# Batched matmul: x loaded one batch per transfer in place of two, and other pieces for the first x's last row tile

## The chip, the cores and the metric

The kernel runs on one core of a Trainium2 chip. The core has a matrix engine (TensorE, PE in the profile; its weight loads are PEld), VectorE (DVE), ScalarE (ACT), GpSimd (POOL) and SyncE (SP), an on-chip memory of 128 partitions (SBUF), an accumulator memory (PSUM), and DMA engines that move data between SBUF and the chip's main memory (HBM). The metric is the time of one execution on the device, in microseconds (us); of several runs the median is given.

## The reference

For each of 32 batches a matrix x[b] of 512 x 1024 is multiplied with a matrix weight[b] of 1024 x 768. Inputs and output are float32 in HBM.

```python
def setup_inputs():
    batch, m, k, n = 32, 512, 1024, 768
    return {
        "x": np.random.randn(batch, m, k).astype(np.float32),
        "weight": np.random.randn(batch, k, n).astype(np.float32),
    }

def reference(x, weight):
    return np.matmul(x, weight).astype(np.float32)
```

A batch reads 2 MiB of x and 3 MiB of weight and writes 1.5 MiB of output. Nothing is shared between batches.

## The kernel before

**Tiling.** P is 128. The 512 rows of a batch are dealt to partitions so that partition p holds rows 4p to 4p+3; each of the four row tiles (MT = 4, index mt) takes one of these rows from every partition. The contraction of 1024 is cut into eight parts of 128 (KT = 8, index ko) in the same interleaved way, so a partition's share of x or of weight is one contiguous run in HBM. Products are computed in bfloat16 and accumulated in float32 PSUM. A row tile has 768 output columns; two row tiles (a pair) fill three PSUM banks of 512 columns, and SPLITS says which piece of which tile goes to which bank.

**Loads.** All loads of weights, and of x from batch 1 on, are issued by GpSimd and turn float32 into bfloat16 on the way. `load_w` (line 65) brings one batch's weights in one transfer, in two or three for the last four batches (CHUNKED). `load_pair` (56) brings x of two batches at once: 64 partitions for each, eight rows to a partition; `load_last` (61) brings the odd last batch alone. x of batch 0 comes as float32 from SP's queue (lines 139 to 144): one transfer for row tiles 0 to 2 over all 128 partitions; for row tile 3, sixteen transfers of six partitions each, four partitions apart, and one of 32 partitions.

**Transposes.** PE needs x with the contraction on the partitions. `words` (73) reads pairs of bfloat16 as one float32 word and transposes them on PE, four 128 x 128 transposes into a PSUM tile pt (two buffers); VectorE copies pt to an xT tile in SBUF. In `transpose_pair` (80) one transposed tile holds rows of both batches of a pair, and the copy sorts them apart; both batches' transposes, eight PSUM tiles, are done ahead of the first batch's matmuls, and the results of the second batch are kept in `ready`. `transpose_first` (97) does batch 0 in float32, eight transposes and two copies for each row tile, all four row tiles ahead of its matmuls. `transpose_last` (90) does batch 31.

**Matmuls and stores.** `matmuls` (117) runs two matmuls for each ko and row tile, 64 a batch. `evacuate` (130) copies the three banks of a pair to the output tile: ScalarE, VectorE, ScalarE. Stores of output are issued by GpSimd one batch behind (line 163), those of batches 25 to 27 together at batch 28; the last four batches' stores are issued by SP (167 to 170 and 203).

**Order.** The whole order is written out by hand. Each engine and each queue takes its instructions in the order of the program: for GpSimd the start is w0, x1 with x2, w1, w2, x3 with x4; then in batch b comes w(b+3) (AHEAD = 3), then the store of b-1, and in odd batches, after the transposes, the pair that begins with x(b+4). A load waits until the buffer that it writes is free: w has four buffers, x two (each of a pair), xT six (each of a pair), output seven. The framework puts in the waits, and gives each queue's DMAs eight semaphores in turn.

Of the kernel before, what the change touches and what calls it, by code (L numbers as in the profile page):

```python
# [9 lines left out]
BF16 = mybir.dt.bfloat16  # L10
# [3 lines left out]
def kernel(  # L14
# [6 lines left out]
    nc = tc.nc  # L21
    B, M, K = x.shape
    _, _, N = weight.shape
    P = 128
    MT = M // P
    KT = K // P
    JT = KT // 2
    N2 = 2 * N
    CHUNKED = {B - 4: (4, 4), B - 3: (4, 4), B - 2: (4, 4), B - 1: (4, 2, 2)}
    AHEAD = 3  # L30
# [3 lines left out]
    const = ctx.enter_context(tc.tile_pool(name="const", bufs=1))  # L34
    first_pool = ctx.enter_context(tc.tile_pool(name="first", bufs=1))
    w_pool = ctx.enter_context(tc.tile_pool(name="w", bufs=4))
    x_pool = ctx.enter_context(tc.tile_pool(name="x", bufs=2))
    xT_pool = ctx.enter_context(tc.tile_pool(name="xT", bufs=6))
    out_pool = ctx.enter_context(tc.tile_pool(name="out", bufs=7))
    tpsum = ctx.enter_context(tc.tile_pool(name="tpsum", bufs=2, space=bass.MemoryType.PSUM))  # L40
    mpsum = ctx.enter_context(tc.tile_pool(name="mpsum", bufs=2, space=bass.MemoryType.PSUM))

    w_view = weight.rearrange("b (ki ko) n -> b ki ko n", ki=P)
    x_view = x.rearrange("b (mi mo) k -> b mi mo k", mi=P)
    pair_view = x[1:B - 1].rearrange("(p r) (mi mo) k -> p (r mi) mo k", r=2, mo=2 * MT)
    out_view = out.rearrange("b (mi mo) n -> b mi (mo n)", mi=P)

    xs, ws, outs = {}, {}, {}

    def banks():
        return [mpsum.tile([P, 512], F32, name=f"pm{i}") for i in range(3)]

    def load_pair(b):

        xs[b] = x_pool.tile([P, 2 * MT, K], BF16, name="x_sb")
        nc.gpsimd.dma_start(out=xs[b], in_=pair_view[b // 2])  # L59

    def load_last():
        xs[B - 1] = x_pool.tile([P, MT, K], BF16, name="x_sb")
        nc.gpsimd.dma_start(out=xs[B - 1], in_=x_view[B - 1])  # L63

    def load_w(b):
        ws[b] = w_pool.tile([P, KT, N], BF16, name="w_sb")
        at = 0
        for n in CHUNKED.get(b, (KT,)):
            nc.gpsimd.dma_start(out=ws[b][:, at:at + n, :], in_=w_view[b, :, at:at + n, :])  # L69
            at += n  # L70


    def words(b, mo):
        pt = tpsum.tile([P, JT, P], F32, name="pt")
        pairs = xs[b].bitcast(F32)
        for j in range(JT):
            nc.tensor.transpose(pt[:, j, :], pairs[:, mo, j::JT], ident)  # L77
        return pt.bitcast(BF16)

    def transpose_pair(b, mt):  # L80

        both = xT_pool.tile([P, 2, JT, P // 2, 2, 2], BF16, name="xT")
        for half in range(2):
            nc.vector.tensor_copy(  # L84
                both[:, :, :, :, half, :].rearrange("p b j i r -> p j b i r"),
                words(b, mt + MT * half).rearrange("p j (b i r) -> p j b i r", b=2, r=2),
            )
        return [both[:, r].rearrange("p j i h r -> p j (i h) r") for r in range(2)]

    def transpose_last(mt):  # L90
        xT = xT_pool.tile([P, JT, P, 2], BF16, name="xT")
        nc.vector.tensor_copy(  # L92
            xT.rearrange("p j m r -> p (j m r)"), words(B - 1, mt).rearrange("p j m -> p (j m)")
        )
        return xT

    def transpose_first(mt):

        xT = xT_pool.tile([P, JT, P, 2], BF16, name="xT")
        for h in range(2):  # L100
            pt = tpsum.tile([P, JT, P], F32, name="pt")
            for i in range(JT):
                nc.tensor.transpose(pt[:, i, :], x_first[:, mt, JT * h + i::KT], ident)  # L103
            nc.vector.tensor_copy(  # L104
                xT[:, 2 * h:2 * h + 2].rearrange("p j m r -> p j r m"),
                pt.rearrange("p (j r) m -> p j r m", r=2),
            )
        return xT
# [8 lines left out]
    def matmuls(pm, half, xT, b, kos, together):  # L117
        for ko in kos:
            for i, (bank, at, off, size) in enumerate(SPLITS[half]):
                shares = half == 1 and i == 0  # L120
                nc.tensor.matmul(  # L121
                    pm[bank][:, at:at + size],
                    xT[:, ko // 2, :, ko % 2],
                    ws[b][:, ko, off:off + size],
                    start=(ko == 0 and not (together and shares)),
                    stop=(ko == KT - 1),
                    skip_group_check=together,
                )

    def evacuate(b, pair, pm):  # L130
        o = outs[b][:, pair * N2:(pair + 1) * N2]
        nc.scalar.copy(o[:, 0:512], pm[0])  # L132
        nc.vector.tensor_copy(o[:, 512:1024], pm[1])  # L133
        nc.scalar.copy(o[:, 1024:N2], pm[2])  # L134

    with tc.manual_schedule():
        x_first = first_pool.tile([P, MT, K], F32)

        nc.sync.dma_start(x_first[:, :MT - 1], x_view[0, :, :MT - 1])
        for block in range(0, 96, 24):  # L140
            for at in range(block, block + 4):
                few = slice(at, block + 24, 4)
                nc.sync.dma_start(x_first[few, MT - 1], x_view[0, few, MT - 1])
        nc.sync.dma_start(x_first[96:, MT - 1], x_view[0, 96:, MT - 1])
        load_w(0)
        ident = const.tile([P, P], F32)
        make_identity(nc, ident)
        load_pair(1)
        load_w(1)
        load_w(2)  # L150
        load_pair(3)

        ready = {}
        pending = []
        for b in range(B):
            if b + AHEAD < B:
                load_w(b + AHEAD)
            if b <= B - LATE:
                if b > 0:
                    pending.append(b - 1)  # L160
                if b + AHEAD < B - HELD or b == B - LATE:
                    for at in pending:
                        nc.gpsimd.dma_start(out=out_view[at], in_=outs[at])  # L163
                    pending = []
            if b == B - 1:
                halves = [slice(pair * N2, (pair + 1) * N2) for pair in range(2)]
                nc.sync.dma_start(out_view[b - 1, :, halves[0]], outs[b - 1][:, halves[0]])
                for late in range(B - LATE, B - 2):
                    nc.sync.dma_start(out_view[late], outs[late])
                nc.sync.dma_start(out_view[b - 1, :, halves[1]], outs[b - 1][:, halves[1]])  # L170
            outs[b] = out_pool.tile([P, MT * N], F32, name="out_sb")
            if b == 0:
                xT = {mt: transpose_first(mt) for mt in range(MT)}
            elif b == B - 1:
                xT = {mt: transpose_last(mt) for mt in range(MT)}
            else:
                if b % 2:
                    for mt in range(MT):
                        ready[b, mt], ready[b + 1, mt] = transpose_pair(b, mt)
                xT = {mt: ready.pop((b, mt)) for mt in range(MT)}  # L180
            if b % 2 and b + AHEAD + 1 < B:
                if b + AHEAD + 1 == B - 1:
                    load_last()
                else:
                    load_pair(b + AHEAD + 1)
            if b not in CHUNKED:
                for pair in range(2):
                    pm = banks()
                    for half in range(2):
                        matmuls(pm, half, xT[2 * pair + half], b, range(KT), False)  # L190
                    evacuate(b, pair, pm)
                continue
            pms = [banks() for _ in range(2)]
            at = 0
            for n in CHUNKED[b]:
                last = at + n == KT
                for mt in range(MT):
                    matmuls(pms[mt // 2], mt % 2, xT[mt], b, range(at, at + n), True)
                    if last and mt % 2 == 1:
                        pair = mt // 2  # L200
                        evacuate(b, pair, pms[pair])
                        if b == B - 1:
                            nc.sync.dma_start(out_view[b, :, halves[pair]], outs[b][:, halves[pair]])
                at += n
# [30 lines left out]
```

## Time and profile before

| What | us |
|---|---|
| median of 3 runs | 521.83 (521.65 to 522.41) |
| the profiled execution's own time | 522.41 |
| its span, first to last instruction | 520.6 |
| PE busy / PE weight loads busy | 428.8 / 276.4 |
| VectorE busy | 131.1 |
| ScalarE busy | 76.2 |
| GpSimd busy | 43.8 |
| first transpose of x_first on PE | 40.43 |
| last evacuation of PSUM ends (ScalarE, line 134) | 506.9 |

The page shows the engines' busy time, then the span in 40 slices of 13 us (each digit is a busy share in tenths; the DMA row is the mean over the core's 16 DMA engines), then the DMA queues: q0 is GpSimd's, q1 SP's, q8 fetches instructions. HBM traffic by the page's count is 167.77 MB read and 50.33 MB written. A stretch's line has the busy time and the number of instructions of each engine, then the granted PE clock, the DMA share and the rate of bytes. A DMA share can lie a little above 1, because packets that follow each other on an engine overlap slightly. A timeline's line has the start, the time taken, the engine, the line and operation, and in brackets how long the engine was idle before it and what ended that. In the chain of waits each line has start, length and what it was, back from the last instruction. The trace also records each DMA packet with its queue, time and size, and the 16 landings of each DMA, one for every DMA engine.

### The profile page before, as it was taken

The page shows a single profiled execution, that of the slowest core. Times are in us where ns is not written, and L with a number is a line of the kernel's source. Part 1 is how long each engine was busy: PE and PEld are TensorE (multiplying, and loading weights), DVE is VectorE, ACT ScalarE, POOL GpSimd, SP SyncE. Part 2 cuts the span into 40 slices and gives each one's busy share as a digit, 9 for nine tenths or more (in the row PEclk, how much of TensorE's full clock was granted, in tenths as well). Part 3 has the DMA queues.
Part 4 walks back from the last instruction along what each step waited for, and adds up shares of the span by engine and source line. Part 5 has one row for each costly group of instructions (what it writes and reads, how often), then busy time and mean ns, then how long its engine had stood idle before and what let it go on. Part 6 is the DMA issues. An engine that isn't in the chain of part 4 may idle for free.

```text
span 520.6 us, 5854 instructions
## 1 busy us (share of the span) xinstructions
PE 428.8 (82%) x2576; PEld 276.4 (53%) x2576; DVE 131.1 (25%) x196; ACT 76.2 (15%) x129; POOL 43.8 (8%) x87
## 2 busy tenths in 40 slices
PE   0008999999999999999896979889797897979980
PEld 0006666666666666666564545465554555646650
DVE  0004515141414232322214132141311414123220
ACT  0000121212111111111020111202011020110210
POOL 3000101001010101000000100010010000101000
PEclk9999999999999999999899989989899998999996
DMA  8999799999999999999999999999999999999996
GB/s 232 224 229 215 148 258 235 307 222 278 278 254 292 215 279 278 267 276 214 287 268 276 282 217 302 244 279 277 243 301 224 276 279 259 292 210 216 283 430 276
DMA packets 12936, 135.63 MB, mean 261 GB/s; under 512 B 1520, under 2 KB 1520, under 8 KB 3312
## 3 DMA queue, kind: packets, MB, share of 16 engines
q0 software_dynamic: 11664, 126.88, 95.7%
q1 hardware_dynamic: 1248, 8.39, 4.0%
q8 instruction: 20, 0.33, 0.2%
q14 instruction: 4, 0.03, 0.0%
HBM read 167.77 MB, written 50.33 MB: 419 GB/s over the span
## 4 chain that ended last, share of the span: by engine, by line
DMA 53%; PE 37%; DVE 4%; another core or an unknown queue 2%; issue 1%; ACT 0%; POOL 0%; POOLq 0%
PE pm L121 30%; DMA w_sb<-in_weight_dram 19%; DMA x_sb<-in_x_dram 18%; DMA out_dram<-out_sb 9%; DMA x_first<-in_x_dram 8%; PE pt L77 6%; DVE xT L84 3%; PE pt L103 1%; DVE out_sb L133 1%; DVE xT L104 0%; DVE xT L92 0%; ACT out_sb L134 0%; POOL out_dram L163 0%; POOLq L163 0%
## 5 line engine op out<-in xcount | busy, mean ns | idle before, releaser
L121 PE MATMUL pm<-w_sb,xT 128*128 128x256 bf16 (+1 forms) x2048 | 338.2, 327 | 8.2 <-DMA w_sb<-in_weight_dram 8.2
L121 PEld LDWEIGHTS <-xT 128*128 128x128 bf16 x2048 | 199.5, 98 | 142.8 <-DMA w_sb<-in_weight_dram 11.4
L133 DVE COPY out_sb<-pm 128x512 f32<-128x512 f32 x64 | 44.3, 692 | 296.8 <-PE pm L121 287.3
L77 PE MATMUL pt<-ident,x_sb 128*128 128x128 f32 x496 | 86.2, 321 | 28.8 <-DMA x_sb<-in_x_dram 20.1
L77 PEld LDWEIGHTS pt<-ident,x_sb 128*128 128x128 f32 x496 | 72.2, 210 | 44.6 <-DMA x_sb<-in_x_dram 23.2
L84 DVE COPY xT<-pt 128x1024 bf16<-128x1024 bf16 x120 | 78.4, 688 | 35.9 <-PE pt L77 35.4
L132 ACT COPY out_sb<-pm 128x512 f32<-128x512 f32 x64 | 37.5, 585 | 307.2 <-PE pm L121 293.5
L134 ACT COPY out_sb<-pm 128x512 f32<-128x512 f32 x64 | 37.5, 585 | 122.8 <-PE pm L121 122.7
L69 POOL DMA_DIRECT2D w_sb<-in_weight_dram x37 | 19.7, 533 | 310.5 <-PE pm L121 183.9
L103 PE MATMUL pt<-ident,x_first 128*128 128x128 f32 x32 | 7.3, 397 | 40.6 <-DMA x_first<-in_x_dram 40.4
L103 PEld LDWEIGHTS pt<-ident,x_first 128*128 128x128 f32 x32 | 5.5, 209 | 42.1 <-issue 40.4
L163 POOL DMA_DIRECT2D out_dram<-out_sb x28 | 15.0, 536 | 68.8 <-DVE xT L84 25.7
L104 DVE CAST xT<-pt 128x512 bf16<-128x512 f32 x8 | 5.9, 737 | 42.7 <-PE pt L103 42.2
L59 POOL DMA_DIRECT2D x_sb<-in_x_dram x15 | 8.0, 532 | 51.1 <-PE pt L77 26.0
L92 DVE COPY xT<-pt 128x1024 bf16<-128x1024 bf16 x4 | 2.6, 686 | 0.2 <-PE pt L77 0.2
L132 ACT ACT_TABLE_LOAD x1 | 1.3, 1283 | 0.7 <-PEq L219 0.7
L63 POOL DMA_DIRECT2D x_sb<-in_x_dram x1 | 0.5, 527 | 3.4 <-DMA w_sb<-in_weight_dram 3.4
masks.py:199 POOL TENSOR_SCALAR_AFFINE_SELECT ident<-ident 128x128 f32<-128x128 f32 x1 | 0.3, 287 | 0.1
masks.py:197 POOL MEMSET ident<- 128x128 f32 x1 | 0.2, 223 | 0.0
L219 POOL MEMSET const-float32-0.0<- 128x1 f32 x1 | 0.1, 98 | 0.2 <-issue 0.2
L219 POOL MEMSET const-bfloat16-1.0<- 128x1 bf16 x1 | 0.1, 101 | 0.0
L219 POOL MEMSET const-uint8-127<- 128x1 uint8 x1 | 0.1, 101 | 0.0
(1 smaller groups left out, 0.1 us busy)
## 6 DMA issues: line engine op xcount, KB each, us to landing
w_sb<-in_weight_dram POOLq DMA_DIRECT2D x28, 1536.0 KB, 41.9
out_dram<-out_sb POOLq DMA_DIRECT2D x28, 1536.0 KB, 42.2
x_sb<-in_x_dram POOLq DMA_DIRECT2D x15, 2048.0 KB, 47.2
w_sb<-in_weight_dram POOLq DMA_DIRECT2D x7, 768.0 KB, 38.6
out_dram<-out_sb SPq DMA_DIRECT2D x4, 768.0 KB
out_dram<-out_sb SPq DMA_DIRECT2D x2, 1536.0 KB
x_first<-in_x_dram SPq DMA_DIRECT2D x1, 1536.0 KB
x_sb<-in_x_dram POOLq DMA_DIRECT2D x1, 1024.0 KB, 36.5
```

Source lines behind the costliest of these rows:

```text
L59: nc.gpsimd.dma_start(out=xs[b], in_=pair_view[b // 2])
L69: nc.gpsimd.dma_start(out=ws[b][:, at:at + n, :], in_=w_view[b, :, at:at + n, :])
L77: nc.tensor.transpose(pt[:, j, :], pairs[:, mo, j::JT], ident)
L84: nc.vector.tensor_copy(both[:, :, :, :, half, :].rearrange("p b j i r -> p j b i r"), words(b, mt + MT * half).rearrange("p j (b i r) -> ...
L92: nc.vector.tensor_copy(xT.rearrange("p j m r -> p (j m r)"), words(B - 1, mt).rearrange("p j m -> p (j m)"))
L103: nc.tensor.transpose(pt[:, i, :], x_first[:, mt, JT * h + i::KT], ident)
L104: nc.vector.tensor_copy(xT[:, 2 * h:2 * h + 2].rearrange("p j m r -> p j r m"), pt.rearrange("p (j r) m -> p j r m", r=2),)
L121: nc.tensor.matmul(pm[bank][:, at:at + size], xT[:, ko // 2, :, ko % 2], ws[b][:, ko, off:off + size], start=(ko == 0 and not (together an ...
L132: nc.scalar.copy(o[:, 0:512], pm[0])
L133: nc.vector.tensor_copy(o[:, 512:1024], pm[1])
L134: nc.scalar.copy(o[:, 1024:N2], pm[2])
L163: nc.gpsimd.dma_start(out=out_view[at], in_=outs[at])
```

## The change

x is loaded one batch to a transfer (`load_x` takes the place of `load_pair` and `load_last`), with five buffers of one batch each. At the start GpSimd's order is w0, x1, w1, x2, w2, x3; in batch b comes x(b+4) first, then w(b+3), then the store of b-1. A batch's transposes are its own: one copy for each row tile, into one of eight xT buffers. Row tiles 0 and 1 are transposed ahead of the matmuls, 2 and 3 between the matmuls of the first pair; batch 0 goes by the same order with `transpose_first`; in the chunked batches each row tile is transposed just ahead of its first matmuls.

Of the first x's last row tile the strided pieces become eight of four partitions, four of five and four of six (partitions 0 to 75), then one of four (76 to 79) and one of 48 (80 to 127). The number of transfers on SP's queue for x of batch 0 goes from 18 to 19.

```diff
-    x_pool = ctx.enter_context(tc.tile_pool(name="x", bufs=2))
-    xT_pool = ctx.enter_context(tc.tile_pool(name="xT", bufs=6))
+    x_pool = ctx.enter_context(tc.tile_pool(name="x", bufs=5))
+    xT_pool = ctx.enter_context(tc.tile_pool(name="xT", bufs=8))
...
-    def load_pair(b):
-
-        xs[b] = x_pool.tile([P, 2 * MT, K], BF16, name="x_sb")
-        nc.gpsimd.dma_start(out=xs[b], in_=pair_view[b // 2])
-
-    def load_last():
-        xs[B - 1] = x_pool.tile([P, MT, K], BF16, name="x_sb")
-        nc.gpsimd.dma_start(out=xs[B - 1], in_=x_view[B - 1])
+    def load_x(b):
+        xs[b] = x_pool.tile([P, MT, K], BF16, name="x_sb")
+        nc.gpsimd.dma_start(out=xs[b], in_=x_view[b])
...
+    def transpose(b, mt):
+
         pt = tpsum.tile([P, JT, P], F32, name="pt")
         pairs = xs[b].bitcast(F32)
         for j in range(JT):
-            nc.tensor.transpose(pt[:, j, :], pairs[:, mo, j::JT], ident)
-        return pt.bitcast(BF16)
...
+            nc.tensor.transpose(pt[:, j, :], pairs[:, mt, j::JT], ident)
         xT = xT_pool.tile([P, JT, P, 2], BF16, name="xT")
         nc.vector.tensor_copy(
-            xT.rearrange("p j m r -> p (j m r)"), words(B - 1, mt).rearrange("p j m -> p (j m)")
+            xT.rearrange("p j m r -> p (j m r)"), pt.bitcast(BF16).rearrange("p j m -> p (j m)")
         )
         return xT
...
         nc.sync.dma_start(x_first[:, :MT - 1], x_view[0, :, :MT - 1])
-        for block in range(0, 96, 24):
-            for at in range(block, block + 4):
-                few = slice(at, block + 24, 4)
-                nc.sync.dma_start(x_first[few, MT - 1], x_view[0, few, MT - 1])
-        nc.sync.dma_start(x_first[96:, MT - 1], x_view[0, 96:, MT - 1])
+        at = 0
+        for few, times in ((4, 2), (5, 1), (6, 1)):
+            for _ in range(times):
+                for first in range(at, at + 4):
+                    rows = slice(first, at + 4 * few, 4)
+                    nc.sync.dma_start(x_first[rows, MT - 1], x_view[0, rows, MT - 1])
+                at += 4 * few
+        for rows in (slice(at, 80), slice(80, P)):
+            nc.sync.dma_start(x_first[rows, MT - 1], x_view[0, rows, MT - 1])
         load_w(0)
...
-        load_pair(1)
-        load_w(1)
-        load_w(2)
-        load_pair(3)
+        for b in range(1, AHEAD):
+            load_x(b)
+            load_w(b)
+        load_x(AHEAD)
...
         for b in range(B):
+            if b + AHEAD + 1 < B:
+                load_x(b + AHEAD + 1)
             if b + AHEAD < B:
                 load_w(b + AHEAD)
...
-            if b == 0:
-                xT = {mt: transpose_first(mt) for mt in range(MT)}
-            elif b == B - 1:
-                xT = {mt: transpose_last(mt) for mt in range(MT)}
-            else:
-                if b % 2:
-                    for mt in range(MT):
-                        ready[b, mt], ready[b + 1, mt] = transpose_pair(b, mt)
-                xT = {mt: ready.pop((b, mt)) for mt in range(MT)}
-            if b % 2 and b + AHEAD + 1 < B:
-                if b + AHEAD + 1 == B - 1:
-                    load_last()
-                else:
-                    load_pair(b + AHEAD + 1)
             if b not in CHUNKED:
+                turn = transpose if b else lambda _, mt: transpose_first(mt)
+                xT = {mt: turn(b, mt) for mt in (0, 1)}
                 for pair in range(2):
                     pm = banks()
                     for half in range(2):
-                        matmuls(pm, half, xT[2 * pair + half], b, range(KT), False)
+                        if pair == 0:
+                            matmuls(pm, half, xT[half], b, range(KT), False)
+                            xT[2 + half] = turn(b, 2 + half)
+                        else:
+                            matmuls(pm, half, xT[2 + half], b, range(KT), False)
                     evacuate(b, pair, pm)
                 continue
+            xT = {0: transpose(b, 0)}
             pms = [banks() for _ in range(2)]
             at = 0
             for n in CHUNKED[b]:
                 last = at + n == KT
                 for mt in range(MT):
+                    if mt + 1 not in xT and mt + 1 < MT:
+                        xT[mt + 1] = transpose(b, mt + 1)
                     matmuls(pms[mt // 2], mt % 2, xT[mt], b, range(at, at + n), True)
```

More of the change, by code (lines that the diff above doesn't have):

```diff
@@ L47 @@
     x_view = x.rearrange("b (mi mo) k -> b mi mo k", mi=P)
-    pair_view = x[1:B - 1].rearrange("(p r) (mi mo) k -> p (r mi) mo k", r=2, mo=2 * MT)
     out_view = out.rearrange("b (mi mo) n -> b mi (mo n)", mi=P)
@@ L70, in load_w @@
             at += n
-    def words(b, mo):
+    def transpose(b, mt):
         pt = tpsum.tile([P, JT, P], F32, name="pt")
@@ L76, in words @@
         for j in range(JT):
-            nc.tensor.transpose(pt[:, j, :], pairs[:, mo, j::JT], ident)
-        return pt.bitcast(BF16)
[L80 to L90, printed above, removed]
+            nc.tensor.transpose(pt[:, j, :], pairs[:, mt, j::JT], ident)
         xT = xT_pool.tile([P, JT, P, 2], BF16, name="xT")
         nc.vector.tensor_copy(
-            xT.rearrange("p j m r -> p (j m r)"), words(B - 1, mt).rearrange("p j m -> p (j m)")
+            xT.rearrange("p j m r -> p (j m r)"), pt.bitcast(BF16).rearrange("p j m -> p (j m)")
         )
@@ L147 @@
         make_identity(nc, ident)
-        load_pair(1)
-        load_w(1)
-        load_w(2)
-        load_pair(3)
-        ready = {}
+        for b in range(1, AHEAD):
+            load_x(b)
+            load_w(b)
+        load_x(AHEAD)
         pending = []
         for b in range(B):
+            if b + AHEAD + 1 < B:
+                load_x(b + AHEAD + 1)
             if b + AHEAD < B:
```

## The prediction

> **What bounds the kernel now.** I read the page first: engine shares, slices, DMA queues.
>
> ```profile
> PE 428.8 (82%) x2576; PEld 276.4 (53%) x2576; DVE 131.1 (25%) x196; ACT 76.2 (15%) x129; POOL 43.8 (8%) x87
> ...
> DMA  8999799999999999999999999999999999999996
> ...
> q0 software_dynamic: 11664, 126.88, 95.7%
> q1 hardware_dynamic: 1248, 8.39, 4.0%
> ```
>
> TensorE has 90 us of idle time, the sixteen DMA engines have almost none: only slice 0, slice 4 (52 to 65 us) and the last slice fall short. The stretches around them say how much:
>
> ```profile
> core 0: us, PE busy (x) PEld busy (x) DVE busy (x) ACT busy (x) POOL busy (x), PEclk, DMA share, GB/s
> ...
> 54.00:56.00 2.00, 2.00 (x15) 1.27 (x13) 0.00 (x0) 0.45 (x1) 0.00 (x0) 1.00 0.67 141
> 56.00:58.00 2.00, 2.00 (x14) 1.22 (x12) 0.00 (x0) 0.14 (x1) 0.00 (x0) 1.00 0.35 76
> 58.00:60.00 2.00, 1.70 (x14) 1.49 (x12) 1.95 (x3) 0.59 (x1) 1.07 (x2) 1.00 0.80 92
> 60.00:62.00 2.00, 1.81 (x13) 1.55 (x13) 1.51 (x4) 0.00 (x0) 0.00 (x0) 1.00 0.49 92
> ...
> 200.00:480.00 280.00, 247.40 (x1465) 157.31 (x1464) 72.39 (x108) 42.14 (x72) 24.93 (x47) 0.96 1.02 261
> ```
>
> From 62 us to 514 us the DMA share is 1.02: the DMA engines set the end, and PE waits for them (88% busy from 200 to 480). The hole at 54 to 62 us is the one place where they ran out of work. Why is in GpSimd's timeline:
>
> ```profile
> 4.57 0.57 POOL L69 DMA_DIRECT2D w_sb<-in_weight_dram  x1
> 58.52 0.53 POOL L69 DMA_DIRECT2D w_sb<-in_weight_dram  x1 [53.39 <-PE pm L121]
> 59.35 0.54 POOL L163 DMA_DIRECT2D out_dram<-out_sb  x1 [0.29 <-issue]
> 64.20 0.53 POOL L59 DMA_DIRECT2D x_sb<-in_x_dram  x1 [4.31 <-PE pt L77]
> ```
>
> All that fits (x1 to x4, w0 to w3) is issued by 4.6 us; w4 needs w0's buffer, thus the end of batch 0 on PE, 53 us later. Batch 0 is late because of the chain of waits:
>
> ```profile
> 0.74 9.42 DMA x_first<-in_x_dram
> ...
> 10.18 15.44 DMA x_first<-in_x_dram
> ...
> 25.64 14.71 DMA x_first<-in_x_dram
> ...
> 40.43 5.87 PE pt L103 x24
> ```
>
> SP has eight semaphores for its DMAs: the 9th waits for the 1st, the 17th for the 9th. PE's first transpose waits for the whole of x_first but the last, unstrided piece.
>
> In the trace's landing records (mean of a DMA's 16 landings, in issue order) the seventh GpSimd load, w3, lands at 56.95, and w4 at 69.44: a step of 12.5 us where w loads otherwise step by 7.27. The hole costs 5.2 us on the mean engine. The same records give the steady prices: pair of x 9.63, single x (the last batch's) 4.86, w 7.27, half of a w 3.66, store of out 3.72. At the end the 16 engines finish the last store between 514.8 and 519.7, mean 516.6: the slowest is 3.1 late.
>
> **The Trainium skill.** "DMA: Bandwidth & Descriptors", section "Queues, rings and completion order": each DMA engine alternates between queues packet by packet. The trace agrees: w and x_first pieces share an engine, and a piece (one data packet, one completion packet) lands every 1.98 us, two w packets of 0.926 plus its own 0.172. The same page, "Why a DMA increments its semaphore by 16 and not by 1": a DMA from SP uses the largest number of engines up to 16 that divides its partitions, the lowest-numbered ones. The records agree on the number: a six-partition piece has six data landings; six engines land w3 2.7 to 3.9 us late. The same page, "Anatomy of one DMA": 2.0 us fixed per GpSimd DMA. In a full queue the trace shows far less (below). "Runtime: NRT & Kernel Launch", section "Instruction fetch mechanics": instructions arrive in 16 KiB blocks; the trace has 20 such packets, 0.94 us each, on the same DMA engines. In the later landings those fetches push back the same eight engines in turn.
>
> **The change part by part.**
>
> *x in single batches.* 15 pair loads become 30 singles: 2 x 4.86 - 9.63 = 0.10 us each, 15 x 0.10 = +1.4 us; from halves of w (2 x 3.66 - 7.27 = 0.06), +0.9. Below zero is excluded, as a packet and a completion more can't shorten a full queue; 15 x 2.0 = 30 us is the page's end of it, if nothing overlapped. I take +1.3, with 0.9 to 4. GpSimd spends 15 x 0.53 us more on issuing, hidden by its 310 us of waiting before w loads alone.
>
> *x(b+4) moved ahead of w(b+3) and out(b-1) in GpSimd's queue; five x buffers.* x5 finds a free buffer, and its semaphore's last user, w0, landed at 14.6; it is queued at about 15 us instead of as a part of the pair issued at 64.20. x_first, x1 to x5 and w0 to w3 end on the mean engine at 56.95 + 4.86 + 0.2 = 62.0. w4 must be issued by about 60.5. Batch 0 ends at 58.0 at the latest (next part), so the hole closes: -5.2 us. Later x(b+4) waits for the transposes of b-1, which finish inside b-1, before the w behind it may go anyway. GpSimd too has eight semaphores: eight outstanding loads now are 2.7 batches of x, w, out (4.86 + 7.27 + 3.72 = 15.85 us), some 42 us of queue, against 50. It stays full.
>
> *x_first.* Sixteen strided pieces before and after; on engines 0 to 3 still two turns each. After the first piece (10.7 us) 15 pieces pass 30 packets of the other queue: before, a pair's packets (1.227) and w's (0.926), until 40.2. Now about 12 of w and 15 of single x at 0.625, completions apart: 11.1 + 9.4 + 15 x 0.172 = 23.1, so about 33.8 us. Batch 0 (two tiles' transposes first, then matmuls: 3.6 + 10.3 + 3.0 = 16.9) ends at about 51, seven earlier. On the end this is worth nothing by itself: DMA is full by then; without it w4 would go at 57.5 to 58.5, still in time.
>
> *What the hole hid.* Lateness goes to the engines carrying the pieces. Before, 16 pieces x (0.172 + 0.02) = 3.1 us on six engines were absorbed by the hole (spread of landings 3.9 at w3, 1.1 at w4). Now 20 data packets and 18 completions on engines 0 to 3 make 3.8 us, engine 4 has 2.1, engine 5 1.3, the others 0.56, mean 1.5: engines 0 to 3 stay 2.3 above the mean to the end. One carrier of pieces took the fetch at 57.2 us (its w3 landing came a further 1.0 late), so carriers and fetch engines overlap at least in part. Fully overlapping, the slowest engine ends some 5.4 after the mean instead of 3.1 (+2.3); disjoint, it stays about 3 or below (0 to -1). I take +1.1.
>
> *PE, DVE.* Same transposes (528) and copies, spread over every batch. Before, a pair's start costs 5.9 us (58.05 to 63.90); now a batch starts matmuls after an evacuation and one copy, 1.4 us, and hides the other tiles: about 12.9 us a batch against 13.2. Cover: w31 lands near 488, PE alone would end near 34 + 32 x 12.9 = 447. Without that cover each us on PE would count. Stores at the end: 31's is issued near 495 instead of 505.65, behind some 20 us of other stores: nothing.
>
> Sum, against the profiled execution (522.41, span 520.6): -5.2 + 1.3 + 1.1 = -2.8. That execution lies 0.6 above the median of 521.83, within the runs' scatter; I put the difference on the median: 521.83 - 2.8 = 519.0.
>
> **Rivals.**
> 1. *Extra pieces on light engines:* the late carriers aren't the fetch engines. -5.2 + 1.3 - 0.3 = -4.2: 517.6. For: up to three of four carriers may be others. Against: one overlap seen.
> 2. *The gain is spent:* full overlap (+2.3) and splits at 0.15 each (+2.3): -0.6, 521.2, no change. For: the single x was priced from one transfer, among loads only.
> 3. *Slower:* beside stores, a separate transfer of 16 KB a partition costs more than 0.26 us extra each, in the stretch from 62 to 480. At that point 15 x 0.26 = 3.9 cancels 5.2 - 1.1; at 0.4 it costs 6.0: -5.2 + 1.1 + 6.0 = +1.9, 523.7. Against: halves of w show 0.06.
> 4. *The pieces don't bring PE forward:* start stays at 40.4; x5 still closes the hole, the same 519.0. Only a start past 44 would reopen it.
>
> **How the numbers follow.** Forecast (rival 4 in it) 0.52, own range 518.2 to 520.2; rival 1 0.26; rival 2 0.12; rival 3 0.10. A measurement of this kernel tells about 0.2%, 1.04 us. Faster 0.78, same 0.12, slower 0.10. The range runs from 516.8 (rival 1 with splits at 0.9 and 0.4 less lateness) to 521.8 (end of rival 2), leaving out rival 3 and a little at both sides.
>
> **What would show it.** Right: no hole near 55 to 62 us, x5's issue near 15 us, PE's first transpose near 34, w4 near 51; x steps of 4.9; a DMA share of 1.0 to about 512; a spread of landings that stays near 3 us after w4 and ends above 4.9. Wrong: x steps above 5.1 beside stores, a new stretch below 0.95, PE waiting in the last 15 us with idle DMA engines, or a last spread that eats over 4 us.

## The result, and the profile after

Six runs of the changed kernel have a median of 516.92 us (516.88 to 517.03), six of the kernel before 522.2 (521.65 to 523.25): a ratio of 0.9898, 95% interval 0.9885 to 0.991. The kernel is faster by 5.3 us, 1.0%. The forecast was 519.0, faster by 2.8, with an own range of 518.2 to 520.2. The measured time lies below that, nearest to rival 1 (517.6), and 0.1 us above the lower end of the whole range (516.8); the gain is nearly twice the forecast one.

The page of the changed kernel, in the lines that answer to those shown of before:

```profile
PE 419.6 (81%) x2576; PEld 275.7 (54%) x2576; DVE 129.8 (25%) x196; ACT 76.2 (15%) x129; POOL 51.7 (10%) x102
...
DMA  8999999999999999999999999999999999999996
...
q0 software_dynamic: 13824, 126.88, 96.7%
q1 hardware_dynamic: 1232, 8.39, 4.1%
```

Slice 4, a 7 before, is a 9. The bytes are the same, in 2160 more packets on q0: 120 on each engine for data (15 transfers x 8) and 15 completions. The same stretches of the changed kernel as before:

```profile
54.00:56.00 2.00, 2.00 (x15) 1.43 (x14) 0.69 (x1) 0.58 (x1) 0.00 (x0) 1.00 1.06 223
56.00:58.00 2.00, 2.00 (x15) 1.45 (x14) 0.00 (x0) 0.24 (x1) 0.00 (x0) 1.00 1.08 227
58.00:60.00 2.00, 2.00 (x15) 1.21 (x14) 1.29 (x2) 0.34 (x1) 0.53 (x1) 1.00 0.98 205
60.00:62.00 2.00, 2.00 (x15) 1.22 (x13) 0.00 (x0) 0.59 (x1) 0.00 (x0) 1.00 1.12 236
...
200.00:480.00 280.00, 240.43 (x1453) 156.71 (x1452) 72.07 (x109) 42.15 (x72) 28.63 (x54) 0.94 1.02 261
```

The hole, with shares of 0.67, 0.35, 0.80 and 0.49 before, is gone; from 200 to 480 us the share is 1.02 as it was, and PE has more idle time than before (240 of 280 us busy against 247). GpSimd's timeline and the chain of waits at the start show what closed the hole:

```profile
15.44 0.53 POOL L56 DMA_DIRECT2D x_sb<-in_x_dram  x1 [9.24 <-DMA w_sb<-in_weight_dram]
50.90 0.53 POOL L62 DMA_DIRECT2D w_sb<-in_weight_dram  x1 [34.93 <-PE pm L101]
51.72 0.54 POOL L148 DMA_DIRECT2D out_dram<-out_sb  x1 [0.28 <-issue]
58.48 0.53 POOL L56 DMA_DIRECT2D x_sb<-in_x_dram  x1 [6.23 <-PE pt L70]
```

```profile
0.74 9.28 DMA x_first<-in_x_dram
...
10.04 10.89 DMA x_first<-in_x_dram
...
20.95 12.60 DMA x_first<-in_x_dram
...
33.64 3.89 PE pt L83 x16
```

x5 goes out at 15.44 us, as soon as w0 has landed; PE starts at 33.6, and w4 goes out at 50.9, when DMA still has work until a mean of 61.9.

### The profile page after: what moved, and what is told of

It reads as the page before. It is cut to its first block, busy times and chain, and to the rows that moved or that the text cites. A ratio compares the mean times of both kernels' runs of the same rounds, so it can differ in the third digit from the quotient of the medians.

```text
span 515.2 us, 6001 instructions
## 1 busy us (share of the span) xinstructions
PE 419.6 (81%) x2576; PEld 275.7 (54%) x2576; DVE 129.8 (25%) x196; ACT 76.2 (15%) x129; POOL 51.7 (10%) x102
## 4 chain that ended last, share of the span: by engine, by line
DMA 69%; PE 25%; DVE 2%; issue 1%; ACT 0%; POOLq 0%
DMA w_sb<-in_weight_dram 31%; PE pm L101 22%; DMA out_dram<-out_sb 16%; DMA x_sb<-in_x_dram 15%; DMA x_first<-in_x_dram 6%; PE pt L70 2%; PE pt L83 1%; DVE out_sb L113 1%; DVE xT L72 1%; ACT out_sb L112 0%; ACT out_sb L114 0%; POOLq L62 0%; POOLq L148 0%; POOLq L56 0%
## 5 line engine op out<-in xcount | busy, mean ns | idle before, releaser
L101 PE MATMUL pm<-w_sb,xT 128*128 128x256 bf16 (+1 forms) x2048 | 364.7, 336 | 47.9 <-DMA w_sb<-in_weight_dram 44.0
L101 PEld LDWEIGHTS <-xT 128*128 128x128 bf16 x2048 | 203.3, 100 | 184.6 <-issue 50.5
L72 DVE COPY xT<-pt 128x1024 bf16<-128x1024 bf16 x124 | 82.8, 689 | 203.0 <-PE pt L70 203.0
L70 PE MATMUL pt<-ident,x_sb 128*128 128x128 f32 x496 | 75.4, 286 | 0.0
L56 POOL DMA_DIRECT2D x_sb<-in_x_dram x31 | 16.5, 532 | 173.4 <-DMA w_sb<-in_weight_dram 129.4
L83 PE MATMUL pt<-ident,x_first 128*128 128x128 f32 x32 | 6.0, 350 | 33.6 <-DMA x_first<-in_x_dram 33.6
L83 PEld LDWEIGHTS pt<-ident,x_first 128*128 128x128 f32 x32 | 5.0, 204 | 34.3 <-issue 33.6
L84 DVE CAST xT<-pt 128x512 bf16<-128x512 f32 x8 | 5.6, 726 | 40.7 <-PE pt L83 40.5
```

The lines of the kernel that those rows point to most:

```text
L56: nc.gpsimd.dma_start(out=xs[b], in_=x_view[b])
L70: nc.tensor.transpose(pt[:, j, :], pairs[:, mt, j::JT], ident)
L72: nc.vector.tensor_copy(xT.rearrange("p j m r -> p (j m r)"), pt.bitcast(BF16).rearrange("p j m -> p (j m)"))
L84: nc.vector.tensor_copy(xT[:, 2 * h:2 * h + 2].rearrange("p j m r -> p j r m"), pt.rearrange("p (j r) m -> p j r m", r=2),)
L101: nc.tensor.matmul(pm[bank][:, at:at + size], xT[:, ko // 2, :, ko % 2], ws[b][:, ko, off:off + size], start=(ko == 0 and not (together an ...
```

## The experiments

Theory H: the whole gain comes from closing the hole; the split of x and the form of the pieces matter only as they close it, and where the pieces land decides only which DMA engine ends last. Its rivals: S, the single loads themselves are better; P, the new pieces are.

A transfer's mean landing is the mean of its landings on the 16 DMA engines; its step is the time from the mean landing of the transfer before it. The table has, from each profiled execution, when PE's first transpose starts, when the first load that waits for a buffer is issued (w4, or x5 where it waits and stands first), by how much that load's step exceeds its usual one (7.30 for w, 4.86 for x), and the mean and the last landing of the last store (the mean is called the mean finish below); then the median of all runs, beside that of the kernel before in the same series. The 0.4 of the two kernels with x_first in one transfer and the 0.56 of the last row are no hole: in the packet records the DMA engines work there without a gap, and the time lies in longer packets just ahead of the first store (last section).

| Kernel | first transpose | load issued | step too long by | mean / last landing | median | before |
|---|---|---|---|---|---|---|
| before | 40.4 | 58.52 | 5.20 | 516.62 / 519.72 | | |
| changed | 33.6 | 50.90 | 0 | 511.17 / 513.45 | 516.92 | 522.2 |
| changed, old pieces | 33.6 | 50.26 | 0 | 511.18 / 514.32 | 517.44 | 522.06 |
| before, new pieces | 40.4 | 58.7 | 5.47 | 517.02 / 520.30 | 522.96 | 522.06 |
| before, x_first in one | 12.3 | 29.75 | 0.41 | 510.81 / 513.81 | 516.69 | 522.06 |
| changed, x_first in one | 12.3 | 29.38 | 0.40 | 511.54 / 513.80 | 516.97 | 522.06 |
| changed, four x buffers | 34.0 | 59.16 | 4.65 | 517.37 / 520.44 | 521.92 | 521.75 |
| the same, x after w | 33.6 | 50.09 | 0 | 511.16 / 513.36 | 516.89 | 521.75 |
| changed, eight of four | 20.9 | 37.37 | 0 | 511.34 / 513.45 | 517.08 | 521.75 |
| before, eight of four | 25.7 | 44.75 | 0 | 511.59 / 513.53 | 517.49 | 521.75 |
| changed, 24 of four | 45.8 | 62.25 | 3.75 | 515.42 / 518.68 | 522.25 | 522.32 |
| changed, 20 of four | 40.7 | 58.27 | 0.56 | 511.78 / 514.78 | 517.19 | 522.32 |

### One part alone

The changed kernel with the old pieces:

```diff
-        for few, times in ((4, 2), (5, 1), (6, 1)):
...
-        for rows in (slice(at, 80), slice(80, P)):
-            nc.sync.dma_start(x_first[rows, MT - 1], x_view[0, rows, MT - 1])
+        for block in range(0, 96, 24):
+            for at in range(block, block + 4):
+                few = slice(at, block + 24, 4)
+                nc.sync.dma_start(x_first[few, MT - 1], x_view[0, few, MT - 1])
+        nc.sync.dma_start(x_first[96:, MT - 1], x_view[0, 96:, MT - 1])
```

> The changed kernel with the old pieces of x_first (sixteen of six partitions, then 32 in one). Theory H (the gain is the closed hole; where x_first's pieces land only decides which DMA engine ends last): PE still starts near 34 us, no hole, w4's mean landing within 0.5 us of the changed kernel's 69.2. The sixth engine, which takes instruction fetches, gets 16 pieces instead of 4, 2.3 us more, and ends last: some 6.5 us after the first instead of 5.05, so +1.2 to +1.6 us, about 518.3. Rival S (the new order of single loads makes the gain, pieces count for nothing): 516.9 within 0.3. Rival P (the new pieces make the gain): back to 521 or more.

Measured: 517.44 (516.35 to 517.46), ratio to before 0.9900 (0.9884 to 0.9917). PE starts at 33.6 and w4 lands at a mean of 69.23: P is out, the old pieces keep the gain. In the profiled execution the last engine is there as expected (the last landing is 3.1 after the mean, against 2.3), but the last landing moved by +0.87 and the median by +0.5, where +1.2 to +1.6 was expected, and two of the five runs lie below all of the changed kernel's.

The kernel before with the new pieces, which is the opposite edit:

> The kernel before with only the new pieces of x_first. Theory H: engines 0 to 3 still have 16 pieces between packets of a pair of x, so PE starts near 40, the hole of about 5 us at 55 to 62 us stays and swallows the pieces' lateness: 522, no change within 0.6. Rival P: 520 or less.

Measured: 522.96 (522.09 to 524.6), ratio 1.0018 (1.0009 to 1.0026). PE starts at 40.4 as before and the hole is there: its step is 5.47 too long. The new pieces gain nothing. That they cost 0.2% was not expected. The profiled executions, 1.0 us apart, show it in parts: the mean finish is 0.40 later, the last landing another 0.19, and the end of the program 0.42, as with the changed kernel's 19th transfer (see "The end" below).

### The hole closed in another way

The kernel before, with its pairs, and the changed kernel, each with x_first in one transfer:

```diff
-        nc.sync.dma_start(x_first[:, :MT - 1], x_view[0, :, :MT - 1])
...
+        nc.sync.dma_start(x_first, x_view[0])
```

> The kernel before, pairs and all, with all of x_first in one transfer over 128 partitions. Theory H: x_first lands near 13 us, PE ends batch 0 near 32, w4 is issued there, no hole: DMA full from 2 us to the end, mean finish about 5.2 us earlier than before, the slowest engine 2.3 to 3 after it: 516.3 to 517.3, the changed kernel's time without a single-batch load. Rival S: the pairs cost something in steady state, so the time stays at 520 or above although the hole is gone.

Measured: 516.69 (516.35 to 517.27), ratio 0.9897 (0.9882 to 0.9912): the changed kernel's time with pairs of x. Its stretches, in the order of those above:

```profile
54.00:56.00 2.00, 2.00 (x15) 1.34 (x14) 0.26 (x1) 0.05 (x1) 0.00 (x0) 1.00 0.96 203
56.00:58.00 2.00, 1.70 (x14) 1.47 (x13) 1.75 (x4) 0.54 (x1) 1.06 (x2) 1.00 1.05 221
58.00:60.00 2.00, 1.81 (x12) 1.44 (x11) 1.75 (x3) 0.00 (x0) 0.00 (x0) 1.00 1.07 227
60.00:62.00 2.00, 1.81 (x13) 1.47 (x13) 1.76 (x4) 0.00 (x0) 0.11 (x1) 1.00 1.06 221
```

No hole. S is out: no single load is needed for the gain.

> The changed kernel with all of x_first in one transfer. Theory H: no hole before, none now, the same work; engines 0 to 3 lose about 2.4 us of pieces each, every other one gets 0.85 more. The last engine of the changed kernel is one of those four at 5.05 after the first, the next at 3.99; so the end moves from 5.05 to about 4.85: -0.2, 516.7 within 0.5. That PE starts some 20 us sooner is worth nothing. Rival: an earlier start of PE is worth time by itself (2 us or more), or the pieces are worth over 1 us as a balance (518 or more).

Measured: 516.97 (516.92 to 517.65), ratio 0.9905 (0.9889 to 0.992). PE starts 21 us earlier than in the changed kernel, for nothing, as DMA is full either way. Against the run with pairs the mean finish is 0.73 later (511.54 and 510.81) and the median 0.28, less than the runs scatter. The split itself shows no price here: from 62 to 480 us a single x steps by 4.83 on average and a pair by 9.66, twice that, where the prediction had 0.06 to 0.10 for each split. (A w steps by 7.33 beside singles and 7.29 beside pairs; why stays open.)

### The hole opened again

The changed kernel with four x buffers:

```diff
-    x_pool = ctx.enter_context(tc.tile_pool(name="x", bufs=5))
+    x_pool = ctx.enter_context(tc.tile_pool(name="x", bufs=4))
```

> The changed kernel with four x buffers in place of five. x5 must now wait for x1's transposes, which end near 57.8 us, and w4 stands behind it in GpSimd's queue although its own buffer is free at 50.4. Theory H: DMA runs dry at a mean of 57.1 us; x5 goes out at 58.5, and as in the kernel before (w4 issued 58.52, landed 10.9 later for a step of 7.3) 3.6 us pass until data flow at full rate: x5 lands near 67 instead of 61.9, all later loads 5 us late: 521 to 522.5. Rival (the smaller transfers or PE's order make the gain, PE starts batch 0 at 34 either way): 517 within 0.5.

Measured: 521.92 (520.72 to 524.26), ratio to before 1.0005 (0.9992 to 1.0017). One buffer less takes the whole gain. Its GpSimd timeline, and the stretch in which DMA has nothing at all:

```profile
59.16 0.53 POOL L56 DMA_DIRECT2D x_sb<-in_x_dram  x1 [52.97 <-PE pt L70]
59.68 0.55 POOL L62 DMA_DIRECT2D w_sb<-in_weight_dram  x1
```

```profile
56.00:58.00 2.00, 2.00 (x14) 1.22 (x13) 0.53 (x1) 0.00 (x0) 0.00 (x0) 1.00 0.27 55
58.00:60.00 2.00, 2.00 (x15) 1.44 (x14) 1.10 (x2) 0.59 (x1) 0.84 (x2) 1.00 0.00 0
```

x5 waits for the last transpose of x1 (line 70), and w4, free since batch 0, waits in the queue behind it. The same four buffers, with x(b+4) issued after w(b+3) and the store:

```diff
-            if b + AHEAD + 1 < B:
-                load_x(b + AHEAD + 1)
             if b + AHEAD < B:
                 load_w(b + AHEAD)
...
+            if b + AHEAD + 1 < B:
+                load_x(b + AHEAD + 1)
```

> Four x buffers as in the run beside it, and the load of x(b+4) moved behind w(b+3) and the store of b-1 in GpSimd's queue. Theory H: w4 goes out at 50.9 us with DMA work left until 57, x5 behind it at about 58, still ahead of the end of w4 at 64 and of the store at 68: no hole, 516.9 within 0.5. So the early start of PE alone is enough, and the fifth buffer matters only because x5 stands before w4. Rival: x loaded later starves PE or leaves DMA short somewhere: 518 or more.

Measured: 516.89 (516.62 to 517.17), ratio 0.9906 (0.989 to 0.9922). Its timeline:

```profile
50.09 0.53 POOL L62 DMA_DIRECT2D w_sb<-in_weight_dram  x1 [43.90 <-PE pm L101]
50.91 0.54 POOL L146 DMA_DIRECT2D out_dram<-out_sb  x1 [0.28 <-issue]
57.68 0.53 POOL L56 DMA_DIRECT2D x_sb<-in_x_dram  x1 [6.23 <-PE pt L70]
```

w4 goes out at 50.1 and the gain is back. So the fifth buffer is needed only because x stands ahead of w in the queue; with the other order PE's earlier start closes the hole alone.

### How late may PE start?

The prediction said that x5 alone closes the hole with PE's start at 40, and that a start past 44 reopens it. The changed kernel with more strided pieces, 24 of four partitions (shown) or 20 (80 in place of 96):

```diff
+        for block in range(0, 96, 16):
+            for at in range(block, block + 4):
+                few = slice(at, block + 16, 4)
+                nc.sync.dma_start(x_first[few, MT - 1], x_view[0, few, MT - 1])
+        nc.sync.dma_start(x_first[96:, MT - 1], x_view[0, 96:, MT - 1])
```

> The changed kernel with 24 strided pieces of four partitions (0 to 95), then one of 32: PE's start is late, all else as in the changed kernel. Eight pieces more pass 16 packets of w2 and x3, about 12.5 us: start near 46, batch 0 ends near 63, w4 goes out at 63.3. With x5 DMA runs dry at a mean of 61.9. In the kernel before and with four x buffers the loss was 3.6 us plus the time from running dry to the issue; so theory H expects 5.0 on w4's step, and the pieces' lateness is swallowed: 521 to 522.5. Rival (PE's start doesn't matter once x5 is queued): 517 to 518.

Measured: 522.25 (520.7 to 523.35), ratio 1.0001 (0.9993 to 1.001). PE starts at 45.8, w4 goes out at 62.25:

```profile
60.00:62.00 2.00, 2.00 (x14) 1.34 (x13) 0.23 (x1) 0.01 (x1) 0.00 (x0) 1.00 0.41 86
62.00:64.00 2.00, 1.64 (x12) 1.21 (x12) 1.74 (x3) 0.57 (x1) 1.06 (x2) 1.00 0.83 117
64.00:66.00 2.00, 2.00 (x15) 1.27 (x13) 0.00 (x0) 0.10 (x1) 0.00 (x0) 1.00 0.69 141
```

The hole stands 4 us later than before, and the gain is gone. w4's step is 3.75 too long where 5.0 was expected, mostly because it went out a microsecond sooner than reckoned.

> The changed kernel with 20 strided pieces of four partitions (0 to 79), then one of 48: PE starts near 40 us, where it started in the kernel before. Batch 0 ends near 57, w4 goes out at 57.3, 4.6 us ahead of running dry at 61.9: theory H says the hole is still closed by x5 alone, w4's mean landing within 0.6 of 69.2; engines 0 to 3 are 0.8 us later than in the changed kernel, so 517 to 518. Rival (the gain is PE's earlier start): 520 to 522.

Measured: 517.19 (517.03 to 518.15), ratio 0.991 (0.9898 to 0.9923).

```profile
58.27 0.53 POOL L62 DMA_DIRECT2D w_sb<-in_weight_dram  x1 [42.35 <-PE pm L101]
```

```profile
58.00:60.00 2.00, 1.65 (x12) 1.24 (x13) 1.76 (x3) 0.59 (x1) 1.06 (x2) 1.00 1.06 221
60.00:62.00 2.00, 2.00 (x15) 1.25 (x13) 0.00 (x0) 0.07 (x1) 0.00 (x0) 1.00 1.08 225
```

PE starts at 40.7, 0.3 later than in the kernel before, and w4 goes out at 58.27, 0.25 earlier; there is no hole and the gain is there: x5 alone is enough.

### Placing the pieces better

Eight pieces of four and one of 96, in the changed kernel and in the kernel before:

```diff
+        for block in (0, 16):
+            for at in range(block, block + 4):
+                few = slice(at, block + 16, 4)
+                nc.sync.dma_start(x_first[few, MT - 1], x_view[0, few, MT - 1])
+        nc.sync.dma_start(x_first[32:, MT - 1], x_view[0, 32:, MT - 1])
```

> The changed kernel with eight strided pieces of four partitions (0 to 31) and one of 96 partitions. Theory H: mean finish as in the changed kernel (511.2); engines 0 to 3 start 1.5 us late instead of 3.2, engines 4 and 5 not at all; the last engine ends some 3.3 us after the first instead of 5.05, near 512.3: -1.1; and with 10 transfers on SP's queue ahead of the six stores the last store's semaphore is again the last that the end of the program waits for, -0.4. 515.4, between 514.9 and 516.2. Rival (where the pieces land is noise): 516.9.

Measured: 517.08 (516.57 to 517.78), ratio 0.991 (0.9893 to 0.9927): a miss. The four engines with the pieces were 1.6 us less late (1.4 to 1.5 behind the first at x4, in place of 3.0 to 3.2), but the last landing is at 513.45, where it was in the changed kernel; it and four others end within 0.8 us.

> The kernel before, pairs of x and all, with the same eight pieces of four and one of 96. Theory H: the last strided piece lands near 25 us, PE ends batch 0 near 43, w4 follows at once, DMA work lasts until 57: no hole. Fifteen fewer transfers than in the changed kernel save 0.7 on the mean finish (between the two kernels with x_first in one transfer it was 511.54 against 510.81), and the last engine is again some 3.3 after the first: 514.8, between 514.2 and 516. Rival: single-batch loads are needed, 517 or more.

Measured: 517.49 (515.43 to 518.83), ratio 0.9919 (0.9896 to 0.9941): outside the expected range. Here pairs finish later than the single loads of the run before (511.59 and 511.34 on the mean), the other way round than with x_first in one transfer. The median lies in the range of the rival, that single loads are needed; but the hole is closed and the time 4.3 us below the kernel before, and with x_first in one transfer pairs have the whole gain. One profile each can't tell such small differences. The runs scatter: they are 3.4 us apart where the changed kernel's are 0.15. One run is the lowest of all, but no version here has a median clearly below the changed kernel's. Relieving the engine that ends last in one profile is no reliable gain; why the runs of this version scatter so much stays open.

## Why the prediction was right, and where its sizes were off

**What bounds the kernel.** Right: the DMA engines, with one hole. Three ways to close it (single loads with five buffers; x_first in one transfer with pairs; four buffers with w first) give 516.69 to 516.92, and three that keep or reopen it 521.92 to 522.96.

**x5 and w4.** Right in each number: x5 near 15 us (15.44), PE's start near 33.8 (33.6), batch 0 ending near 51 (w4 at 50.9), DMA work until 62.0 (61.9), hole closed (w4's step 7.30, -5.2). The working of the pieces by turns of the two queues held.

**Split transfers.** This term was too large: +1.3 was taken, from one single load among loads. Between the two kernels the mean finish moved by -5.45, of which the hole is -5.2, so that splits and all else together cost nothing. From 62 to 480 us a single x steps by 4.85 on average (median 4.82), two of them 0.01 (medians) to 0.09 (means) above a pair, but a store steps by 3.71 on average instead of 3.76. The two other comparisons of single loads with pairs, at the same pieces, have the mean finish 0.73 later and 0.25 earlier. The 2.0 us fixed per DMA that the Trainium skill states ("DMA: Bandwidth & Descriptors", "Anatomy of one DMA") don't appear where the queue is full; rival 3 with its 0.26 or more is out.

**What the hole hid.** This step failed, and with its sign: +1.1 was taken for the lateness of the engines with pieces, and the last landing is 2.28 after the mean instead of 3.10, so -0.8. The lateness stayed, as forecast. These are the offsets of the 16 landings from the first, sorted, in the changed kernel's landing records, with the time of the first landing:

```
x4, 48.6 us    0.00 ... 0.46 0.72 1.34 3.01 3.05 3.09 3.20
w3, 55.9 us    0.00 ... 0.49 1.33 1.81 3.00 3.04 3.08 3.18
out0, 71.7 us  0.00 ... 0.51 1.46 1.47 1.83 3.03 3.06 3.10 3.22
x7, 92.4 us    0.00 ... 0.46 1.33 1.34 1.55 1.83 3.01 3.06 3.10 3.21
```

The records don't name the engine; which is which is read from how many pieces it carries. The first row has the four engines with all the pieces (3.0 to 3.2), the fifth, with eight (1.34), and the sixth, with four (0.72). The instruction fetch at 49.9 us pushes the sixth to 1.81, those at 69.6 and 91.3 two engines with hardly any pieces; the ninth, at 222, takes the one at 1.8 on to 2.9. The four are moved only by a few smaller fetches of 8 KB. So the lateness fell on engines that the 16 KB fetches leave alone, and evened the end: this is rival 1, whose mechanism held. The overlap that the prediction saw before the result was real, but by these records it was the sixth engine, which carried 16 pieces then and carries four now; with the old pieces one of six late engines goes from 2.9 to 3.9 with the fetch at 49.1 us, and the last landing is 0.87 later. The engine that ends last in the changed kernel is still one of the four: 8 KB fetches at 119.7, 294.2 and 476.3 us take it from 3.2 to 4.0, 4.6 and 5.05.

**The end.** A term of the sum that was missing: the changed kernel's span ends 1.80 after its last landing, before 0.92. With 19 transfers on SP's queue in place of 18 the last store's semaphore is the first of eight that the end of the program waits for, and the other waits follow it (0.43); GpSimd's last steps take 0.45 longer, for a reason that was not tried. -5.45 - 0.82 + 0.88 = -5.4, the spans' difference (520.6 to 515.2). That the time lies in the range at all is in part luck: without this missing term the two terms before, both taken too large, would have carried it to about 516.0, below the range.

**PE.** Right: its earlier start is worth nothing by itself. Where the hole is closed, PE starts anywhere between 12 and 41 us for the same time.

## What to carry to other kernels

Where DMA is full from end to end but for one hole, price the hole and look for the instruction that stands first in the issuing queue then: what it waits for, and what is ready behind it. Here a buffer more was enough (20 pieces), and so was a start of PE 28 us earlier (pairs, x_first in one transfer); a start 7 us earlier was not, until the order in the queue was changed with it (four x buffers). Then ask what the hole had hidden, engine by engine: a late DMA engine, once nothing lets it catch up, stays late to the end.

## What was not expected

A load issued to DMA engines that have run dry costs more than the dry time. In the kernel before, w4 was issued 1.57 us after the mean engine had landed its last packet, and its step was 5.20 too long (3.6 on top); with 24 pieces 0.34 and 3.75 (3.4); with four x buffers 2.06 and 4.65 (2.6).

The packet records show where this goes. The Trainium skill ("DMA: Bandwidth & Descriptors", "Latency and other measured facts") gives about 1 us to the first byte of a GpSimd DMA; here the first packet starts 1.2 us after the issue in all three runs. Then the first packet or two of each engine take up to 2.25 us; a packet of w otherwise takes 0.93 and one of a single x 0.62. That costs 0.82, 0.60 and 0.72 us an engine.

Another part has to do with the first store. In these three runs the last packets of w4, just ahead of the first store, take up to 1.8 us, which costs 1.14, 0.83 and 0.79 us an engine. (With four x buffers this is the load behind x5, whose step is 0.9 too long.) So the hole's 5.2 us have 1.1 of this kind in them, and what a dry queue costs on top of the dry time is 2.5 to 2.6 in each of the three. The same long packets stand there in three runs without a hole: 0.40 and 0.41 us an engine with x_first in one transfer, 0.57 with 20 pieces; in the changed kernel there are none. What sets them off stays open.

With 20 pieces w4 was issued 3.7 us ahead of running dry, and its first packets are of the usual length, so that this was early enough. How much later it might have gone out was not tried.
